# Diagonal of a 2-D prefix sum: rows kept in fp32, loaded uncast in 384-row strips, three rows per partition added before the matmul

## The chip, the cores and the metric

The kernel runs on one core of one Trainium2 chip. The metric is the device time in microseconds (us), lower is better; a time quoted for a kernel is the median of its runs.

The profiles show one execution each. Their span, from the first to the last instruction, is shorter than the time of the same run, and the profile before is of a run of 667.14 us, below the median; so spans are compared with spans and times with times.

## The reference

```python
def setup_inputs():
    B, H, W = 4, 4224, 4224
    return {"x": np.random.randn(B, H, W).astype(np.float32)}

def reference(x):
    ps = np.cumsum(np.cumsum(x, axis=1), axis=2)
    diag = np.diagonal(ps, axis1=1, axis2=2)
    return np.cumsum(diag, axis=1).astype(np.float32)
```

Element i of the diagonal is the sum of the square x[:i+1, :i+1], and the output is a running sum of that: 4 x 4224 numbers out of 285.5 MB. Every element of x has to be read once; the rest is adding. Rows left of the diagonal enter as row sums, columns above it as column sums, and the blocks on the diagonal are split by a triangular mask.

## The kernel before

Four matrices are read in strips of 768 rows (six rows per partition), cast from fp32 to bf16 by the DMA on GpSimd's queue, into three buffers. TensorE adds up columns: a one-hot selector `sel` puts the 128 partitions' sum into one row of a PSUM tile `d`, one matmul for each of the six rows and each 384 columns. VectorE masks the diagonal block and makes the row sums next to it; ScalarE makes the row sums further left (`act_sum`).

```python
    def load_rows(o, b, r0):
        f = o.shape[1]
        nc.gpsimd.dma_start(
            out=o, in_=x[b, r0 : r0 + f * P, :].rearrange("(p f) w -> p f w", f=f)
        )
    # ... (cut)
        def add_up(strip, f, r0, acc, um, wp=0, ws=None):
            # ... (cut)
            for j in range(g + nw, NG):
                for q in range(f):
                    columns(j, 0, GW, strip[:, q, j * GW : (j + 1) * GW])
            # ... (cut)
            block = strip[:, :, r0:hi]
            nc.vector.tensor_mul(out=mu, in0=block, in1=um)
            nc.vector.tensor_sub(out=block, in0=block, in1=mu)
            for q in range(f):
                for h in range(nw):
                    columns(g + h, 0, GW, mu[:, q, h * GW : (h + 1) * GW])
                if ws > wp:
                    act_sum(acc[:, q, 0:1], strip[:, q, wp:ws])
            row_sums(acc[:, :, 1], strip[:, :, ws:hi])
```

In the tail (the last 384 rows, in pieces) bf16 matmuls with an identity (`fold_in`) add up columns for VectorE, before the fp32 matmuls `fin_a`, `fin_b` and `fin_e` weigh the last sums together:

```python
        fold_in(fold_a, part_a, *acuts[1], 256)
        row_sums(asum[:, :, 3], fold_a)
        arows = last.tile([P, 2], FP32, name="arows")
        row_sums(arows, asum)
```

Of the kernel before, what the change touches and what calls it, by code (L numbers as in the profile page):

```python
# [8 lines left out]
FP32 = mybir.dt.float32  # L9
# [8 lines left out]
def kernel(  # L18
# [14 lines left out]

    nc = tc.nc
# [5 lines left out]
    F2 = 2 * F  # L40
# [7 lines left out]
    NS = NG // 2  # L48
# [17 lines left out]


    HC = GW
    NH = N - HC
    src = x[LB, T0:N, :].rearrange("(h p) w -> p h w", p=P)  # L70
    src_a = src[:, 0:2, :]
    head = last.tile([P, F, HC], FP32, name="head")
    nc.sync.dma_start(out=head, in_=src[:, :, NH:N])

    def strip_tile():
        return strips.tile([P, F2, N], BF16, name="strip")

    def load_rows(o, b, r0):
        f = o.shape[1]
        nc.gpsimd.dma_start(  # L80
            out=o, in_=x[b, r0 : r0 + f * P, :].rearrange("(p f) w -> p f w", f=f)
        )

    prefetched = []
    for i in range(NBUF):
        t = strip_tile()
        load_rows(t, 0, i * F2 * P)
        prefetched.append(t)


    sel = consts.tile([P, 2 * NW - 1], BF16, name="sel")
    nc.vector.memset(sel, 0.0)
    nc.vector.memset(sel[:, NW - 1 : NW], 1.0)

    um_all = consts.tile([P, (F2 * F2 + F * F + F) * P], BF16, name="um")
    nc.vector.memset(um_all, 1.0)  # L96

    def upper_mask(f, c0):

        um = um_all[:, c0 : c0 + f * f * P].rearrange("p (q c) -> p q c", q=f)  # L100
        nc.gpsimd.affine_select(  # L101
            out=um,
            in_=um,
            compare_op=ALU.is_gt,
            fill=0.0,
            base=0,
            pattern=[[-1, f], [1, f * P]],
            channel_multiplier=-f,
        )
        return um  # L110

    um6 = upper_mask(F2, 0)
    um3 = upper_mask(F, F2 * F2 * P)
    um1 = um_all[:, (F2 * F2 + F * F) * P :]
    nc.gpsimd.affine_select(
        out=um1,
        in_=um1,
        compare_op=ALU.is_gt,
        fill=0.0,
        base=0,  # L120
        pattern=[[1, GW]],
        channel_multiplier=-1,
    )

    ones_all = consts.tile([P, P + 1 + GW], FP32, name="ones_all")
    nc.vector.memset(ones_all, 1.0)
    ident = ones_all[:, :P]
    ones_col = ones_all[:, P : P + 1]
    ones_row = ones_all[:NW, P + 1 :]
# [9 lines left out]

    HP = P // 2  # L140
    halves = consts.tile([P, HP], FP32, name="halves")
    nc.gpsimd.tensor_add(out=halves, in0=ident[:, :HP], in1=ident[:, HP:])

# [78 lines left out]
    ident_h = consts.tile([P, P], BF16, name="ident_h")  # L222
    nc.vector.tensor_copy(out=ident_h, in_=ident)

# [5 lines left out]
    weights4_h = consts.tile([P, P], BF16, name="weights4_h")  # L230
    nc.vector.tensor_copy(out=weights4_h, in_=weights4)

    def fold_in(o, src, c0, c1, w, start=False):

        for c in range(c0, c1, w):
            matmul(o, ident_h, src[..., c : c + w], start=start and c == c0)

    def act_sum(acc, src):
        w = src.shape[-1]
        dump = dumpool.tile([P, 2176], BF16, name="dump")  # L240
# [7 lines left out]
    pairs = []  # L248

    def pair_sum(acc, src):  # L250

        w = src.shape[-1] // 2
        pair = last.tile([P, 288], FP32, name=f"pair{len(pairs)}")
        pairs.append(pair)
# [8 lines left out]
        )  # L263

# [11 lines left out]
    def scalar_cols(r0):  # L276

        return r0 * 9 // 16 // 32 * 32



    rows6, rows3 = [], []
    for i, n in enumerate((NW, NG)):
        rows6.append(consts.tile([P, n + 1, F2], FP32, name=f"rows6_{i}"))
        rows3.append(consts.tile([P, n, F], FP32, name=f"rows3_{i}"))
        nc.vector.memset(rows6[i], 0.0)
        nc.vector.memset(rows3[i], 0.0)


    asum = last.tile([P, 2, 4], FP32, name="asum")  # L290
# [262 lines left out]
```

## Time and profile before

| | before |
|---|---|
| time, median of the first 3 runs | 668.9 us (667.1 to 668.97) |
| span of the profile | 665.4 us |
| read from HBM | 285.47 MB |
| last full strip of 384 rows landed | 648.76 us |
| VectorE busy, instructions counted | 326.4 us, 136 |

The lines on which the prediction rests are in it, below. The order of reading is: which engine or queue is full, then the chain of waits for what releases what, then the tail.

### The profile page before, as it was taken

How to read it: one execution, taken by the hardware profiler on the slowest of the kernel's cores; microseconds unless marked ns; L12 is line 12 of the kernel's file. 1: busy time of each engine (PE TensorE's matmuls, PEld its weight loads, DVE VectorE, ACT ScalarE, POOL GpSimd, SP SyncE). 2: the span in 40 equal slices, each digit the busy share in tenths (PEclk: the TensorE clock that was granted, in tenths of full speed). 3: DMA queues.
4: the chain of work that ended last, by engine and by line, in shares of the span. 5: the costliest groups of instructions: out<-in, count | busy, mean ns of one | idle time of the engine just before them, and what ended most of it. 6: DMA issues, size and time to landing. Idle time of an engine off the chain costs nothing.

```text
span 665.4 us, 2461 instructions
## 1 busy us (share of the span) xinstructions
PE 201.7 (30%) x948; PEld 103.7 (16%) x948; DVE 326.4 (49%) x136; ACT 136.9 (21%) x222; POOL 31.8 (5%) x62
## 2 busy tenths in 40 slices
PE   0081423402007143140200623404032163250418
PEld 0040211201004021120100312202011031120103
DVE  3261625456906153454780524436388243352767
ACT  0001121406300103040630020304063002030434
POOL 6100000000000000000000000000000000001000
PEclk9995857656558585666755957666565586766758
DMA  9999999999999999999999999999999999999998
GB/s 206 219 219 219 219 219 215 212 210 218 219 218 219 219 220 218 218 213 212 216 218 218 217 219 219 218 219 211 215 216 219 219 214 220 216 219 216 214 208 162
DMA packets 7631, 143.25 MB, mean 215 GB/s; under 512 B 536, under 2 KB 1604, under 8 KB 2116
## 3 DMA queue, kind: packets, MB, share of 16 engines
q0 software_dynamic: 7152, 142.44, 99.9%
q1 hardware_dynamic: 468, 0.66, 0.3%
q8 instruction: 7, 0.11, 0.1%
q14 instruction: 4, 0.03, 0.0%
HBM read 285.47 MB, written 0.07 MB: 429 GB/s over the span
## 4 chain that ended last, share of the span: by engine, by line
another core or an unknown queue 44%; DVE 42%; DMA 11%; issue 1%; POOL 0%; PE 0%; DVEq 0%; POOLq 0%
DVE acc L246 27%; DMA strip<-in_x_dram 11%; DVE mu L333 7%; DVE strip L334 7%; DVE c L440 0%; POOL strip L411 0%; DVE rows L348 0%; PE d L226 0%; POOL strip L400 0%; DVE pu L246 0%; PE fin_e L226 0%; DVE c L266 0%; DVE pair L255 0%; PE carry_ps L226 0%
## 5 line engine op out<-in xcount | busy, mean ns | idle before, releaser
L226 PE MATMUL d<-strip,sel 128*33 128x384 bf16 (+1 forms) x603 | 140.7, 408 | 397.9 <-DMA strip<-in_x_dram 397.9
L241 ACT ACTIVATE dump<-strip 128x416 bf16<-128x416 bf16 (+6 forms) x110 | 125.1, 1138 | 520.5 <-DMA strip<-in_x_dram 517.8
L333 DVE TENSOR_TENSOR mu<-strip,um 128x4608 bf16<-128x4608 bf16 (+1 forms) x24 | 52.4, 2183 | 316.4 <-DMA strip<-in_x_dram 316.3
L246 DVE TENSOR_REDUCE acc<-strip 128x6 f32<-128x4608 bf16 (+6 forms) x23 | 196.0, 8523 | 0.8
L226 PEld LDWEIGHTS <-sel 128*33 128x33 bf16 (+1 forms) x849 | 94.9, 112 | 534.1 <-issue 495.9
L226 PE MATMUL d<-mu,sel 128*33 128x384 bf16 (+1 forms) x243 | 48.9, 353 | 45.4 <-DVE mu L333 45.4
L334 DVE TENSOR_TENSOR strip<-strip,mu 128x4608 bf16<-128x4608 bf16 (+1 forms) x24 | 52.4, 2183 | 1.0
L80 POOL DMA_DIRECT2D strip<-in_x_dram x24 | 16.5, 687 | 536.7 <-DVE acc L246 312.3
L241 ACT ACTIVATION_READ_ACCUMULATOR dump<-strip 128x1 f32 x110 | 20.5, 186 | 0.0
L226 PE MATMUL fold<-strip,ident_h 128*128 128x480 bf16 x8 | 3.4, 601 | 10.8 <-DMA strip<-in_x_dram 10.8
L96 DVE MEMSET um<- 128x6144 bf16 x1 | 5.2, 5178 | 1.2 <-issue 1.2
L216 DVE TENSOR_SCALAR steps<-steps 128x128 int32<-128x128 int32 x1 | 0.2, 227 | 11.0 <-POOL steps L215 11.0
L101 POOL TENSOR_SCALAR_AFFINE_SELECT um<-um 128x4608 bf16<-128x4608 bf16 (+1 forms) x2 | 5.2, 2614 | 4.0 <-DVE um L96 4.0
L226 PEld LDWEIGHTS <-ident_h 128*128 128x128 bf16 x21 | 2.2, 113 | 14.8 <-issue 13.8
L411 POOL DMA_DIRECT2D strip<-in_x_dram x5 | 2.7, 552 | 26.5 <-DMA strip<-in_x_dram 26.5
L226 PE MATMUL d<-ones_all,rows 128*33 128x128 f32 (+1 forms) x12 | 2.3, 347 | 5.4 <-DVE rows L348 5.4
L226 PE MATMUL fold_a<-strip,ident_h 128*128 128x512 bf16 x13 | 3.3, 380 | 0.3 <-DMA strip<-in_x_dram 0.3
L246 DVE TENSOR_REDUCE parts<-strip 128x3 f32<-128x3072 bf16 x1 | 3.4, 3352 | 0.0
L400 POOL DMA_DIRECT2D strip<-in_x_dram x2 | 1.4, 714 | 30.8 <-DVE acc L246 30.8
L226 PEld LDWEIGHTS d<-halves,rows 128*33 128x33 f32 (+1 forms) x24 | 2.5, 150 | 0.7 <-issue 0.5
L226 PE MATMUL d<-halves,rows 128*33 128x64 f32 (+1 forms) x24 | 2.6, 284 | 0.0
L348 DVE TENSOR_TENSOR rows<-acc 64x30 f32<-64x30 f32 (+2 forms) x12 | 2.1, 177 | 0.9
(80 smaller groups left out, 34.7 us busy)
## 6 DMA issues: line engine op xcount, KB each, us to landing
strip<-in_x_dram POOLq DMA_DIRECT2D x19, 6336.0 KB, 76.6
strip<-in_x_dram POOLq DMA_DIRECT2D x5, 3168.0 KB, 59.8
strip<-in_x_dram POOLq DMA_DIRECT2D x1, 1152.0 KB, 50.2
strip<-in_x_dram POOLq DMA_DIRECT2D x1, 768.0 KB, 53.3
strip<-in_x_dram POOLq DMA_DIRECT2D x3, 240.0 KB, 54.3
head<-in_x_dram SPq DMA_DIRECT2D x1, 576.0 KB, 4.0
strip<-in_x_dram POOLq DMA_DIRECT2D x1, 176.0 KB, 43.2
strip<-in_x_dram POOLq DMA_DIRECT2D x1, 64.0 KB, 28.6
```

What stands on the lines that cost most here:

```text
L80: nc.gpsimd.dma_start(out=o, in_=x[b, r0 : r0 + f * P, :].rearrange("(p f) w -> p f w", f=f))
L96: nc.vector.memset(um_all, 1.0)
L101: nc.gpsimd.affine_select(out=um, in_=um, compare_op=ALU.is_gt, fill=0.0, base=0, pattern=[[-1, f], [1, f * P]], channel_multiplier=-f,)
L216: nc.vector.tensor_single_scalar(out=steps, in_=steps, scalar=2, op=ALU.arith_shift_right)
L226: nc.tensor.matmul(o, lhsT=lhsT, rhs=rhs, start=start, stop=False, skip_group_check=True)
L241: nc.scalar.activation(out=dump[:, :w], in_=src, func=ACT.Copy, accum_out=acc)
L246: nc.vector.reduce_sum(out=acc, in_=src, axis=AX.X)
L333: nc.vector.tensor_mul(out=mu, in0=block, in1=um)
L334: nc.vector.tensor_sub(out=block, in0=block, in1=mu)
L348: nc.vector.tensor_add(out=o, in0=acc[..., 0], in1=acc[..., 1])
L400: nc.gpsimd.dma_start(out=part_a[:, :, c0:c1], in_=src_a[:, :, c0:c1])
L411: nc.gpsimd.dma_start(out=part_b[:, sb, c0:c1], in_=x[b, r0 : r0 + R, :NH].rearrange("r (k c) -> r k c", k=4)[:, :, c0:c1],)
```

## The change

The intent is to drop the cast and the software queue, and to keep full fp32 precision: SyncE loads strips of 384 rows (three rows per partition) as they are. An fp32 matmul takes more time for a column than a bf16 one (in the trace of before it is recorded twice, at 0.82 ns a column each, against 0.42 once), so VectorE adds the three rows first and TensorE then needs a third of the matmuls. The mask is made of -1 and 0, and a second selector, `minus_sel`, turns the sign.

```diff
     def load_rows(o, b, r0):
-        f = o.shape[1]
-        nc.gpsimd.dma_start(
-            out=o, in_=x[b, r0 : r0 + f * P, :].rearrange("(p f) w -> p f w", f=f)
+        nc.sync.dma_start(
+            out=o, in_=x[b, r0 : r0 + GW, :].rearrange("(p f) w -> p f w", f=F)
         )
 ... (cut)
-            for j in range(g + nw, NG):
-                for q in range(f):
-                    columns(j, 0, GW, strip[:, q, j * GW : (j + 1) * GW])
-            nc.vector.tensor_mul(out=mu, in0=block, in1=um)
-            nc.vector.tensor_sub(out=block, in0=block, in1=mu)
-            row_sums(acc[:, :, 1], strip[:, :, ws:hi])
 ... (cut)
+            for q in range(F):
+                act_sum(acc[:, k, q, 0:1], strip[:, q, :ws])
+            for q in range(F):
+                block = strip[:, q, g * GW : hi]
+                masked(mu[:, q, :], block, um3[:, q, :], acc[:, k, q, 2:3])
+            for q in range(1, F):
+                add_to(mu[:, 0, :], mu[:, q, :])
+            columns(g, mu[:, 0, :], minus_sel)
+            if hi < N:
+                for q in range(1, F):
+                    add_to(strip[:, 0, hi:], strip[:, q, hi:])
+                for j in range(g + 1, NG):
+                    columns(j, strip[:, 0, j * GW : (j + 1) * GW])
+            for q in range(F):
+                pair_sum(acc[:, k, q, 1:2], strip[:, q, ws:hi])
 ... (cut: in the tail)
-        fold_in(fold_a, part_a, *acuts[1], 256)
-        row_sums(asum[:, :, 3], fold_a)
+        sum_a(3, *acuts[1], acuts[1][0] + 768)
```

`sum_a` does with ScalarE and VectorE what the bf16 `fold_in` matmuls did.

More of the change, by code (lines that the diff above doesn't have):

```diff
@@ L39 @@
     F = 3
-    F2 = 2 * F
     GW = P * F
@@ L47 @@
     NBUF = 3
-    NS = NG // 2
     NW = NG * LB
@@ L64 @@
     ctx.enter_context(tc.manual_schedule())
-    HC = GW
-    NH = N - HC
-    src = x[LB, T0:N, :].rearrange("(h p) w -> p h w", p=P)
-    src_a = src[:, 0:2, :]
-    head = last.tile([P, F, HC], FP32, name="head")
-    nc.sync.dma_start(out=head, in_=src[:, :, NH:N])
     def strip_tile():
-        return strips.tile([P, F2, N], BF16, name="strip")
+        return strips.tile([P, F, N], FP32, name="strip")
     def load_rows(o, b, r0):
-        f = o.shape[1]
-        nc.gpsimd.dma_start(
-            out=o, in_=x[b, r0 : r0 + f * P, :].rearrange("(p f) w -> p f w", f=f)
+        nc.sync.dma_start(
+            out=o, in_=x[b, r0 : r0 + GW, :].rearrange("(p f) w -> p f w", f=F)
         )
@@ L86, with selector @@
         t = strip_tile()
-        load_rows(t, 0, i * F2 * P)
+        load_rows(t, 0, i * GW)
         prefetched.append(t)
-    sel = consts.tile([P, 2 * NW - 1], BF16, name="sel")
-    nc.vector.memset(sel, 0.0)
-    nc.vector.memset(sel[:, NW - 1 : NW], 1.0)
-    um_all = consts.tile([P, (F2 * F2 + F * F + F) * P], BF16, name="um")
-    nc.vector.memset(um_all, 1.0)
-    def upper_mask(f, c0):
-        um = um_all[:, c0 : c0 + f * f * P].rearrange("p (q c) -> p q c", q=f)
+    NH = N - GW
+    src = x[LB, T0:N, :].rearrange("(h p) w -> p h w", p=P)
+    src_a = src[:, 0:2, :]
+    head = last.tile([P, F, GW], FP32, name="head")
+    nc.sync.dma_start(out=head, in_=src[:, :, NH:N])
+    def selector(name, value):
+        t = consts.tile([P, 2 * NW - 1], FP32, name=name)
+        nc.vector.memset(t, 0.0)
+        nc.vector.memset(t[:, NW - 1 : NW], value)
+        return t
+    um3 = consts.tile([P, F, GW], BF16, name="um3")
+    um1 = consts.tile([P, GW], BF16, name="um1")
+    for um, pattern, cm in (
+        (um3, [[-1, F], [1, GW]], -F),
+        (um1, [[1, GW]], -1),
+    ):
+        nc.vector.memset(um, -1.0)
         nc.gpsimd.affine_select(
@@ L106, in upper_mask @@
             base=0,
-            pattern=[[-1, f], [1, f * P]],
-            channel_multiplier=-f,
-        )
-        return um
-    um6 = upper_mask(F2, 0)
-    um3 = upper_mask(F, F2 * F2 * P)
-    um1 = um_all[:, (F2 * F2 + F * F) * P :]
-    nc.gpsimd.affine_select(
-        out=um1,
-        in_=um1,
-        compare_op=ALU.is_gt,
-        fill=0.0,
-        base=0,
-        pattern=[[1, GW]],
-        channel_multiplier=-1,
-    )
-    ones_all = consts.tile([P, P + 1 + GW], FP32, name="ones_all")
+            pattern=pattern,
+            channel_multiplier=cm,
+        )
+    sel = selector("sel", 1.0)
+    minus_sel = selector("minus_sel", -1.0)
+    ones_all = consts.tile([P, P + GW], FP32, name="ones_all")
     nc.vector.memset(ones_all, 1.0)
     ident = ones_all[:, :P]
-    ones_col = ones_all[:, P : P + 1]
-    ones_row = ones_all[:NW, P + 1 :]
+    ones_row = ones_all[:NW, P:]
     nc.gpsimd.affine_select(
@@ L138 @@
     )
-    HP = P // 2
-    halves = consts.tile([P, HP], FP32, name="halves")
-    nc.gpsimd.tensor_add(out=halves, in0=ident[:, :HP], in1=ident[:, HP:])
     def counted(name, rows, width, pieces):
@@ L220 @@
     nc.vector.tensor_scalar_max(out=weights4, in0=steps, scalar1=0.0)
-    ident_h = consts.tile([P, P], BF16, name="ident_h")
-    nc.vector.tensor_copy(out=ident_h, in_=ident)
     def matmul(o, lhsT, rhs, start=False):
@@ L228, in matmul @@
         )
-    weights4_h = consts.tile([P, P], BF16, name="weights4_h")
-    nc.vector.tensor_copy(out=weights4_h, in_=weights4)
-    def fold_in(o, src, c0, c1, w, start=False):
-        for c in range(c0, c1, w):
-            matmul(o, ident_h, src[..., c : c + w], start=start and c == c0)
     def act_sum(acc, src):
         w = src.shape[-1]
-        dump = dumpool.tile([P, 2176], BF16, name="dump")
+        dump = dumpool.tile([P, 2688], BF16, name="dump")
         nc.scalar.activation(
@@ L246, in row_sums @@
         nc.vector.reduce_sum(out=acc, in_=src, axis=AX.X)
-    pairs = []
     def pair_sum(acc, src):
         w = src.shape[-1] // 2
-        pair = last.tile([P, 288], FP32, name=f"pair{len(pairs)}")
-        pairs.append(pair)
+        pair = dumpool.tile([P, 1024], BF16, name="pair")
         nc.vector.scalar_tensor_tensor(
@@ L263, in pair_sum, with add_to @@
         )
+    def add_to(o, i):
+        nc.vector.tensor_add(out=o, in0=o, in1=i)
     def masked(o, i, m, acc):
@@ L274, in masked @@
         )
-    def scalar_cols(r0):
-        return r0 * 9 // 16 // 32 * 32
-    rows6, rows3 = [], []
+    accs = []
     for i, n in enumerate((NW, NG)):
-        rows6.append(consts.tile([P, n + 1, F2], FP32, name=f"rows6_{i}"))
-        rows3.append(consts.tile([P, n, F], FP32, name=f"rows3_{i}"))
-        nc.vector.memset(rows6[i], 0.0)
-        nc.vector.memset(rows3[i], 0.0)
-    asum = last.tile([P, 2, 4], FP32, name="asum")
+        accs.append(consts.tile([P, n, F, 3], FP32, name=f"acc{i}"))
+        nc.gpsimd.memset(accs[i], 0.0)
+    asum = last.tile([P, 2, 5], FP32, name="asum")
     dtot = last.tile([P, F], FP32, name="dtot")
@@ L293, with do_head @@
     hu = last.tile([P, 3], FP32, name="hu")
-    hmu = last.tile([P, 3, GW], BF16, name="hmu")
-    row_sums(hs, head)
-    for h in range(F):
-        w = GW - h * P
-        masked(hmu[:, h, :w], head[:, h, HC - w :], um1[:, :w], hu[:, h : h + 1])
-    nc.vector.tensor_sub(out=dtot, in0=hs, in1=hu)
-    nc.gpsimd.tensor_copy(out=asum[:, :, 0], in_=dtot[:, 0:2])
+    hmu = last.tile([P, F, GW], FP32, name="hmu")
+    def do_head():
+        row_sums(hs, head)
+        for h in range(F):
+            w = GW - h * P
+            masked(
+                hmu[:, h, GW - w :], head[:, h, GW - w :], um1[:, :w], hu[:, h : h + 1]
+            )
+        for h in range(1, F):
+            add_to(hmu[:, 0, h * P :], hmu[:, h, h * P :])
+        nc.vector.tensor_add(out=dtot, in0=hs, in1=hu)
+        nc.vector.tensor_copy(out=asum[:, :, 0], in_=dtot[:, 0:2])
     for b in range(B):
         whole = b < LB
-        r6, r3 = rows6[b // LB], rows3[b // LB]
+        acc = accs[b // LB]
         if b in (0, LB):
@@ L311, in row_of, with columns @@
             return b * NG + j if whole else (j + 1) % NG
-        def columns(j, lo, hi, rhs):
+        def columns(j, rhs, s=sel):
             k = row_of(j)
-            lhsT = sel[:, NW - 1 - k : NW - 1 - k + rows]
-            matmul(d[:, lo:hi], lhsT, rhs, start=first[0])
+            matmul(d, s[:, NW - 1 - k : NW - 1 - k + rows], rhs, start=first[0])
             first[0] = False
-        def add_up(strip, f, r0, acc, um, wp=0, ws=None):
-            nw = f * P // GW
-            g = r0 // GW
-            hi = r0 + f * P
-            for j in range(g + nw, NG):
-                for q in range(f):
-                    columns(j, 0, GW, strip[:, q, j * GW : (j + 1) * GW])
-            if ws is None:
-                ws = scalar_cols(r0)
-            mu = mup.tile([P, f, f * P], BF16, name=f"mu{f}")
-            block = strip[:, :, r0:hi]
-            nc.vector.tensor_mul(out=mu, in0=block, in1=um)
-            nc.vector.tensor_sub(out=block, in0=block, in1=mu)
-            for q in range(f):
-                for h in range(nw):
-                    columns(g + h, 0, GW, mu[:, q, h * GW : (h + 1) * GW])
-                if ws > wp:
-                    act_sum(acc[:, q, 0:1], strip[:, q, wp:ws])
-            row_sums(acc[:, :, 1], strip[:, :, ws:hi])
@@ L342, with add_up @@
-        acc6 = smalls.tile([P, NS, F2, 2], FP32, name="acc6")
-        acc3 = smalls.tile([P, 2, F, 2], FP32, name="acc3")
-        nc.vector.memset(acc6[:, 0, :, 0], 0.0)
-        def sum_up(o, acc):
-            nc.vector.tensor_add(out=o, in0=acc[..., 0], in1=acc[..., 1])
-        ns = NS if whole else NS - 1
-        for s in range(ns):
+        def add_up(strip, g, ws):
+            k = row_of(g)
+            hi = (g + 1) * GW
+            mu = mup.tile([P, F, GW], FP32, name="mu")
+            for q in range(F):
[13 more added lines that the diff above has]
+                pair_sum(acc[:, k, q, 1:2], strip[:, q, ws:hi])
@@ L352 @@
+        for g in range(NG if whole else LG):
             strip = prefetched.pop(0) if prefetched else None
@@ L354 @@
                 strip = strip_tile()
-                load_rows(strip, b, s * F2 * P)
-            add_up(strip, F2, s * F2 * P, acc6[:, s], um6)
-            if not whole and s == 1:
-                for h in range(F):
-                    columns(LG, h * P, GW, hmu[:, h, : GW - h * P])
-        a6 = acc6[:, :ns]
-        for h in range(2):
-            ps = slice(h * HP, (h + 1) * HP)
-            k = row_of(h)
-            sum_up(r6[ps, k : k + 2 * ns : 2, :], a6[ps])
-        strip = strip_tile()
-        if whole:
-            load_rows(strip[:, :F], b, T0)
-            add_up(strip[:, :F], F, T0, acc3[:, 0], um3)
-            sum_up(r3[:, row_of(LG), :], acc3[:, 0])
-        else:
-            for h in range(2):
-                load_rows(strip[:, h * F : h * F + F], b, T0 - (2 - h) * GW)
-            add_up(strip[:, :F], F, T0 - 2 * GW, acc3[:, 0], um3)
-            sum_up(r3[:, row_of(LG - 2), :], acc3[:, 0])
-            fold_g = psum_s.tile([P, F, 160], FP32, name="fold")
-            wp, ws = 1280, 1280 + 1536
-            fold_in(fold_g, strip[:, F:], 0, wp, 160, start=True)
-            parts = last.tile([P, F, 3], FP32, name="parts")
-            add_up(strip[:, F:], F, T0 - GW, parts, um3, wp, ws)
-            row_sums(parts[:, :, 2], fold_g)
-            row_sums(r3[:, row_of(LG - 1), :], parts)
+                load_rows(strip, b, g * GW)
+            hi = (g + 1) * GW
+            add_up(strip, g, hi * 5 // 8 // 32 * 32)
+            if b == 0 and g == NBUF - 1:
+                do_head()
+            if not whole and g == 1:
+                columns(LG, hmu[:, 0, :], minus_sel)
         if b < LB - 1:
             continue
-        for q in range(F2):
-            matmul(d[:, q : GW : F2], r6[:, :rows, q], halves)
+        r3 = last.tile([P, rows, F], FP32, name=f"r3_{rows}")
+        row_sums(r3, acc)
         for q in range(F):
@@ L399 @@
             for c0, c1 in acuts:
-                nc.gpsimd.dma_start(out=part_a[:, :, c0:c1], in_=src_a[:, :, c0:c1])
+                nc.sync.dma_start(out=part_a[:, :, c0:c1], in_=src_a[:, :, c0:c1])
             CB = NH // 4
@@ L410 @@
                 r0 = TB + sb * R
-                nc.gpsimd.dma_start(
+                nc.sync.dma_start(
                     out=part_b[:, sb, c0:c1],
@@ L416, with sum_a @@
                 )
-            fold_a = psum_s.tile([P, 2, 256], FP32, name="fold_a")
-            c0, c1 = acuts[0]
-            cp, ca = c0 + 1792, c0 + 1792 + 256
-            fold_in(fold_a, part_a, c0, c0 + 1280, 256, start=True)
-            for h in range(2):
-                act_sum(asum[:, h, 1:2], part_a[:, h, cp:ca])
-            row_sums(asum[:, :, 2], part_a[:, :, ca:c1])
+            def sum_a(k, c0, c1, ca):
+                for h in range(2):
+                    act_sum(asum[:, h, k : k + 1], part_a[:, h, c0:ca])
+                for h in range(2):
+                    pair_sum(asum[:, h, k + 1 : k + 2], part_a[:, h, ca:c1])
+            sum_a(1, *acuts[0], acuts[0][0] + 1536)
         pu = last.tile([rows, 2], FP32, name=f"pu{rows}")
@@ L434 @@
         matmul(carry_ps[:, 1:2], apart, pu[:, 0:1])
-        if not whole:
-            fold_in(fold_a, part_a, c0 + 1280, cp, 256)
         carry = last.tile([rows, 2], FP32, name=f"carry{rows}")
@@ L448 @@
         if whole:
-            to = out[0:LB, :].rearrange("b (g i) -> (b g) i", i=GW)
-            nc.sync.dma_start(out=to, in_=c12[:, 1, :])
+            c12_w = c12
             continue
+        to = out[0:LB, :].rearrange("b (g i) -> (b g) i", i=GW)
+        nc.sync.dma_start(out=to, in_=c12_w[:, 1, :])
         nc.sync.dma_start(
@@ L482, in finish @@
             )
-        by_ps = psum_s.tile([P, P], FP32, name="fold")
-        for c in range(0, CB, P):
-            w = min(P, CB - c)
-            matmul(by_ps[:w], part_b[:, 0, c : c + w], weights4_h, start=c == 0)
-        by = last.tile([P, P], FP32, name="by")
-        nc.scalar.copy(out=by, in_=by_ps)
         weigh_b(dtot[:, 2:3], weights, M0, start=True)
@@ L494 @@
             weigh_a(arows[:, h : h + 1], h * P, start=h == 0)
-        weigh_b(ones_col, by, M0)
         for h in range(2):
             weigh_b(arows[:, h : h + 1], weights, h * P)
-        bsum = last.tile([P, 2, 2], FP32, name="bsum")
-        for k, ca in ((0, 480), (1, 416)):
-            act_sum(bsum[:, k, 0:1], part_b[:, k + 1, :ca])
-            pair_sum(bsum[:, k, 1:2], part_b[:, k + 1, ca:])
-        finish(fin_a, 0, M0)
-        for k in range(2):
+        bsum = last.tile([P, 3, 2], FP32, name="bsum")
+        for k, ca in ((0, 480), (1, 480), (2, 416)):
+            act_sum(bsum[:, k, 0:1], part_b[:, k, :ca])
+            pair_sum(bsum[:, k, 1:2], part_b[:, k, ca:])
+            if k == 1:
+                finish(fin_a, 0, M0)
+        for k in range(3):
             for i in (1, 0):
-                weigh_b(bsum[:, k, i : i + 1], weights4, M0 + (k + 1) * R)
+                weigh_b(bsum[:, k, i : i + 1], weights4, M0 + k * R)
         esum = last.tile([P, 3], FP32, name="esum")
```

## The prediction

> **What bounds the kernel now.** I read the summary of the span first, then the slices and the DMA queues, then the chain of waits in order of time, then the groups kept apart by shape, and last the timeline of the final 20 us.
>
> ```profile
> PE 201.7 (30%) x948; PEld 103.7 (16%) x948; DVE 326.4 (49%) x136; ACT 136.9 (21%) x222; POOL 31.8 (5%) x62
> ...
> DMA  9999999999999999999999999999999999999998
> ...
> q0 software_dynamic: 7152, 142.44, 99.9%
> q1 hardware_dynamic: 468, 0.66, 0.3%
> ...
> HBM read 285.47 MB, written 0.07 MB: 429 GB/s over the span
> ```
>
> No engine is busy for more than half of the span, while the 16 DMA engines are full in every slice. 142.44 MB were written (bf16) but 285.47 MB read (fp32), so the cast halves only the side that lands in SBUF. The chain of waits gives the rate:
>
> ```profile
> 1.33 33.28 DMA strip<-in_x_dram
> 34.64 2.57 DVE mu L333
> 37.23 2.57 DVE strip L334
> 39.83 4.95 DVE acc L246
> 44.78 19.74 another core or an unknown queue
> 64.62 2.57 DVE mu L333
> ...
> 364.70 2.57 DVE mu L333
> ...
> 529.11 2.57 DVE mu L333
> ```
>
> VectorE starts on a strip of 768 rows, works for 10 us, then waits 20 us until the next has landed; the wait that the chain calls an unknown queue is the one that the table of waits calls DVE mu waiting for DMA strip (316.3 us in 20 waits). From 364.70 to 529.11 one whole matrix goes by: 4224 x 4224 x 4 bytes = 71.37 MB in 164.41 us, which is 434.1 GB/s read. The half strips of 384 rows are no slower: one and a half strips take 44.87 us (155.25 to 200.12), one 29.9. So the end of the kernel is: first landing at 34.6, a stream at 434 GB/s, and what follows the last landing:
>
> ```profile
> 648.76 0.76 DVE L333 TENSOR_TENSOR mu<-strip,um 128x1152 bf16<-128x1152 bf16 x1 [5.42 <-DMA strip<-in_x_dram]
> ...
> 655.65 0.55 DVE L246 TENSOR_REDUCE pu<-d 11x1 f32<-11x384 f32 x1 [0.53 <-PE d L226]
> ...
> 662.33 0.38 DVE L255 SCALAR_TENSOR_TENSOR pair<-strip 128x208 f32<-128x208 bf16 x1
> ```
>
> The last strip lands at 648.7, the tail pieces behind it (13.6 us of stream) keep VectorE waiting for data until 662.3, and the span ends at 665.4: only 3 us lie after the last byte, 16.7 us after the last strip.
>
> **What the Trainium skill says.** "DMA: Bandwidth & Descriptors", section "Where 436 GB/s comes from", puts the ceiling of the 16 engines' ports at 435.2 GB/s. The trace agrees: 434.1 on the read side, so there is nothing left to gain in the stream. The trace does not show a long stream that also writes at that rate, since the cast writes half. The same page, section "iDMA fabric", has a load stream from the SyncE queue, alone, at 408.7 GB/s, with 1 MiB per DMA and rows of 4 KiB. Here one 6.5 MB DMA has 50,688 contiguous bytes per partition; if the missing 6% is a cost per row or per DMA, it shrinks to well under 1%; if it is the price of writing what is read, it stays. "VectorE: DVE Perf Modes", section "The perf-mode tier table", gives an fp32 tensor_tensor one element per cycle, against two in bf16; the second is in the trace (1152 bf16 in 758 ns, 4608 in 2558: 0.52 ns each and 158 ns fixed). "Vector Engine (DVE) Microarchitecture Reference", section "Points that are easy to get wrong", says that the scalar-tensor-tensor form with two SBUF sources that are not bf16 runs at half rate; no such instruction is in the trace (the mask is bf16, pairs are bf16), so this is open.
>
> **The change part by part.** The bytes read stay the same. Loads go from 24 strip DMAs on the GpSimd queue to 43 on the SyncE queue, 6.49 MB each, 6.49/434 = 14.95 us each. Three buffers of 50,688 bytes per partition hold three such strips, as before in bytes, so the stream runs 30 us ahead of the strip at work instead of 60. What a strip g (0 to 10) now costs must fit in 14.95 us per engine, and its buffer must be free 29.9 us after it landed.
>
> ```profile
> L226 PE MATMUL d<-strip,sel 128*33 128x384 bf16 x450 | 104.7, 407 | 320.0 <-DMA strip<-in_x_dram 320.0
> ...
> L246 DVE TENSOR_REDUCE acc<-strip 128x6 f32<-128x10752 bf16 x4 | 45.4, 11353 | 0.1
> ...
> L241 ACT ACTIVATE dump<-strip 128x2144 bf16<-128x2144 bf16 x9 | 17.9, 1990 | 13.4 <-DMA strip<-in_x_dram 13.2
> ...
> L266 DVE SCALAR_TENSOR_TENSOR hmu<-head,um 128x384 bf16<-128x384 f32 x1 | 0.5, 547 | 0.0
> ...
> L226 PE MATMUL fin_a<-weights,arows 128*1 128x256 f32 x2 | 0.6, 377 | 0.2 <-DVE arows L246 0.2
> ...
> L226 PE MATMUL fin_a<-weights,arows 128*1 128x128 f32 x2 | 0.4, 272 | 0.0
> ```
>
> VectorE loses the reductions (196 us) and the bf16 mask multiply and subtract (105 us). One element costs 1.042 ns (the reductions of 4608 and 10752 differ by 6400 ns) and an instruction about 157 ns. Per strip it gains: three masked products, 3 x (0.547 + 0.08 accumulator read) = 1.9; two adds of 384, 2 x 0.557 = 1.1; two adds of 3840-384g, for g=0 2 x 4.157 = 8.3; three pair sums of 80 to 800, 0.24 x 3 = 0.7 at g=0 plus 0.24 for reads, 3.2 at g=10. Sum 12.3 us at g=0, 9.4 at g=5, 6.2 at g=10; at half rate of the pair sums 12.5, 10.8, 8.7. All under 14.95. Over the kernel: 81 + 48 + 189 + 88 and 15 of small work, about 420 us, or 478 at half rate.
>
> ScalarE: a sum over ws costs 0.833 ws + 0.39 us with its read; three of 2624 make 7.7 us, the kernel some 205 us.
>
> TensorE: fp32 matmuls appear twice each in the trace, at 0.82 ns per column (377-272 over 128), twice the 0.42 of bf16, so four bf16 passes. In the first strip 66 bf16 matmuls took 13.6 us at a granted clock of 0.75, 0.155/clock each; fp32 then is 0.62/clock, 0.94 us at the mean clock 0.66 and 1.24 at 0.5. But VectorE first adds three rows, so their number falls from 846 to 264, at most 11 per strip: 10.3 to 13.6 us. PE busy would be 200 to 270 us. The buffer of strip 0 is free at 3 + 8.3 + 10 x 0.94 = 21 us after landing, 24 at the low clock, so the next load is queued 6 to 9 us before the queue runs dry. Nothing here enters the path.
>
> GpSimd loses 20 us of issuing, off the path. At the start SyncE issues at 0.8 instead of 1.3; the head load (issued 0.8, landed 4.0 us later, of which 1.4 is bytes) shows some 2.2 us of latency, so strip 0 lands near 18.0. The rest of the stream, 279.0 MB, ends at 660.8 at 434 GB/s (before: 662.3).
>
> The tail is where work reaches the path. After the last strip lands at T, VectorE now does in order: that strip (g=9: 1.9+1.1+1.1+3.0 = 7.1), the sum of parts and matmuls (1.4), pair sums of the tail (1.3), pu and mask (1.2), carry (0.6), two scans (2.05), pair sums (1.5), three short pairs and an add (2.0), two pairs (0.8), the last matmuls, add and store (1.2). It ends near T+18.2; the tail pieces land by T+14.5. So VectorE, not the last byte, ends it: 1.5 us later than the 16.7 of before, 5 at half rate. T is 660.8-13.6 = 647.2, the span 665.4 or 669. Times are 3.5 us above the span (668.9 against 665.4; the profiled run itself 1.7). That makes 669 to 672 at an unchanged rate; at 430 GB/s, 6 more.
>
> **Rivals.** (1) The stream loses where it also writes 434 GB/s. At 425: 285.5/0.425 is 14 us more, so about 684; at 408.7 it is 41 us more, 711. For it: no margin at the port ceiling, and the skill's figure. Against it: its rows are a twelfth of these, and the head load, also fp32 and uncast in 1,536-byte rows, took 40.4% of 5 us x 16 engines for 0.59 MB, 292 GB/s, above the 217 that the cast stream writes, so writing is not bounded there. (2) VectorE or the four-pass matmuls become the bound on early strips, or hold buffers longer than 29.9 us. At 12.5 against 14.95 it would take 20% more than reckoned; then only strips 0 and 1 of each matrix would exceed it, some 1 to 3 us each, up to 10 us in all. (3) The cast or the software queue costs something now and its loss speeds the stream up. Against it: 434.1 of 435.2 leaves 0.3%, 2 us. (4) All is hidden and the time is unchanged to 0.5%, the case reckoned above.
>
> **Range and chances.** Most weight is on 668 to 676; a moderate loss of rate (425 to 430) puts 676 to 684; a fifth I give to a loss that exceeds 2% (above 682.3). I put 673, and 664 to 694 to hold it 8 times in 10. Faster by over 2% would need 655.5, less than the read side allows: 0.02. Within 2%: 0.77. Slower: 0.21.
>
> **What would show each step.** DMA again 9 in all slices, and starts of successive strips 14.95 us apart: rate kept; 15.3 or more with DMA still full: rival 1. DVE at 63% (or 72%: half rate, seen in pair sums of 720 at 1.66 us rather than 0.91). PE under 45%, and waits of SyncE's loads for PE or DVE that end before the queue is empty; DMA slices under 9 would mean rival 2. Strip 0 landing at 18. Some 18 to 22 us from the last strip's landing to the end, with VectorE busy throughout. The prediction fails if long fp32 rows stream below 425 GB/s or a strip needs over 14.95 us on one engine.

## More of the kernel before

On the page of before, the columns are packets, MB and the share of 16 engines' time:

```profile
q8 instruction: 7, 0.11, 0.1%
q14 instruction: 4, 0.03, 0.0%
```

They bring the engines' own instructions, in pieces of 16,384 bytes (q8) and 8,192 bytes (q14).

## The result, and the profile after

The changed kernel took 677.26 us (676.84 to 677.95, 4 runs) against 668.05 for the kernel before in the same rounds. A ratio is the mean time of one kernel's fast runs over that of the other's fast runs of the same rounds, so it isn't quite the ratio of these medians: 1.0139, with a 95% interval of 1.0118 to 1.016. That is within 2%, but it is a real loss of 9 us.

The page of the kernel after:

```profile
span 675.7 us, 2520 instructions
...
PE 281.8 (42%) x576; PEld 70.3 (10%) x576; DVE 387.9 (57%) x738; ACT 198.0 (29%) x275; POOL 7.1 (1%) x30
...
DMA  9999999999999999999999999999999999999993
...
q1 hardware_dynamic: 7924, 285.55, 98.2%
...
q14 instruction: 10, 0.08, 0.0%
HBM read 285.47 MB, written 0.07 MB: 423 GB/s over the span
```

The DMA engines are still full up to the last slice, which reads 3 where before it read 8; and VectorE is over half busy at most. So the stream still bounds the kernel, but it moves fewer bytes per us over the span (423 against 429 GB/s), and the end is longer. To see where, one follows the landings. ScalarE waits for each strip in this kernel, so its starts are the landings. The timeline of ScalarE, after (start, duration, what; in brackets the idle time before and what ended it):

```profile
276.89 1.59 ACT L214 ACTIVATE dump<-strip 128x1664 bf16<-128x1664 f32 x1 [10.45 <-DMA strip<-in_x_dram]
...
292.86 1.80 ACT L214 ACTIVATE dump<-strip 128x1920 bf16<-128x1920 f32 x1 [10.86 <-DMA strip<-in_x_dram]
...
307.85 1.99 ACT L214 ACTIVATE dump<-strip 128x2144 bf16<-128x2144 f32 x1 [9.24 <-DMA strip<-in_x_dram]
...
655.68 2.20 ACT L214 ACTIVATE dump<-strip 128x2400 bf16<-128x2400 f32 x1 [8.75 <-DMA strip<-in_x_dram]
```

From 292.86 to 307.85 is 14.99 us, and nearly all strips are that far apart: 6.49 MB in 14.99 us, 433 GB/s. But from 276.89 to 292.86 is 15.97 us. Six of the 42 intervals are such long ones, ending near 66, 172, 293, 414, 520 and 626 us (the first also holds the head load). The last strip lands at 655.68 instead of 648.76, 6.9 us later.

What happened in the long intervals is in the trace's single DMA packets. They don't name their engine, so I chained them: a packet that starts within 20 ns of another's end is taken to be on the same engine, which gives 16 chains. One of these chains around 282 us, from my own listing of the records:

```
start us   took      bytes   queue
280.088   1875 ns   50688   q1
281.959    325 ns    8192   q14   (instructions)
282.272   2534 ns   50688   q1
284.803   1874 ns   50688   q1
```

An instruction piece takes 0.33 us of that engine, and the data packet behind it takes 0.66 us longer than its neighbours: 0.98 us lost on one of 16 engines, which is the excess of the interval. Pieces at 55.1, 161.0, 282.0, 402.9, 508.8 and 614.7 us lie on the same chain, each with a packet of 2534 or 2535 ns behind it. A strip is there only when all 16 engines have brought their share, so this engine's delays add up: at the end its last packet of the last strip ends at 655.06 us, those of the other 15 chains between 648.6 and 650.5. Pieces of the other engines fall on other chains, one or two each, and stay inside that lag. (In the kernel before, the pieces are spread over different chains, as far as the chaining there can be trusted.)

The Trainium skill, "Runtime: NRT & Kernel Launch", section "Instruction fetch mechanics", says that each engine's instruction memory is a queue which is refilled in blocks by a DMA queue of the sequencer, and takes the cost as mostly hidden from the engine. The trace agrees on the engine: no wait of VectorE is put down to it. What it shows in addition is that the stream of data pays. The spacing fits VectorE: the trace has 795 instructions on it with those for semaphores, and 795 / 128 is 6.2 pieces (8,192 bytes for 128 instructions is the skill's proportion, 16 KiB for 256).

After the last strip, the chain of waits of the kernel after (start, duration, the engine and tile that the end waited for):

```profile
655.68 2.31 ACT dump L214 x2
...
662.66 0.26 DVE r L219
...
668.73 0.17 DVE arows L219
...
668.94 1.44 PE fin_a L207 x4
670.38 2.79 PE fin_b L207 x16
...
673.58 0.18 DVE ye L449
```

and its counterpart in the chain of the kernel before:

```profile
663.29 0.18 DVE ye L521
```

The end comes 2.1 us after `ye` in both (the store). In the kernel after, the three sums of ScalarE hold the first 7.0 us, VectorE the next 6.1, then TensorE 4.6 until `ye`. The windows of both kernels tell why TensorE is slow there. The columns are us, then busy time and count of PE, PEld, DVE, ACT and POOL, then PE's granted clock, the DMA share and GB/s. After, then before:

```profile
666.00:669.00 3.00, 0.06 (x1) 0.06 (x2) 2.83 (x8) 2.91 (x7) 0.00 (x0) 0.50 0.09 32
669.00:672.00 3.00, 3.00 (x13) 1.53 (x14) 2.08 (x11) 1.41 (x6) 0.00 (x0) 0.50 0.01 4
```

```profile
658.00:661.00 3.00, 2.79 (x19) 1.33 (x19) 2.45 (x6) 0.96 (x3) 0.00 (x0) 1.00 1.13 204
```

TensorE did next to nothing from 666 to 668.94 and then ran at clock 0.50; before, it was busy with the bf16 folds and ran at 1.00. Also, the DMA share is 0.09 and 0.01 here: the data had ended but for the engine that lagged.

The difference of the spans, 675.7 - 665.4 = 10.3 us, as I add it up (the parts make 10.5):

| part | us | how |
|---|---|---|
| start | 0.85 | two strips were in at 34.13 and the head's bytes took 1.36 more; before, the same bytes were in at 34.64 |
| rate | 1.9 | 42 strips x (14.99 - 14.945) |
| instruction pieces | 4.4 | 636.55 - 42 x 14.99 - 1.36 = 5.6 in the stretch from strip 0 to the last, against 1.2 of irregular intervals before |
| tail | 3.4 | 20.0 us from the last strip's landing to the end, against 16.6 |

### The profile page after: what moved, and what is told of

Read it like the earlier page. It is cut to its first block, busy times and chain, and to the rows that moved or that the text cites. A ratio compares the mean times of both kernels' runs of the same rounds, so it can differ in the third digit from the quotient of the medians.

```text
span 675.7 us, 2520 instructions
## 1 busy us (share of the span) xinstructions
PE 281.8 (42%) x576; PEld 70.3 (10%) x576; DVE 387.9 (57%) x738; ACT 198.0 (29%) x275; POOL 7.1 (1%) x30
## 4 chain that ended last, share of the span: by engine, by line
DMA 72%; DVE 13%; PE 11%; ACT 2%; issue 1%; SPq 0%; DVEq 0%; ACTq 0%
DMA strip<-in_x_dram 72%; PE d L207 10%; DVE strip L236 8%; DVE mu L239 2%; ACT dump L214 2%; DVE mu L236 2%; PE fin_b L207 0%; DVE pair L225 0%; DVE c L377 0%; PE fin_a L207 0%; SPq L69 0%; DVE c L239 0%; DVE pu L219 0%; DVE yl L416 0%; DVE r L219 0%
## 5 line engine op out<-in xcount | busy, mean ns | idle before, releaser
L214 ACT ACTIVATE dump<-strip 128x224 bf16<-128x224 f32 (+13 forms) x137 | 184.0, 1343 | 453.4 <-DMA strip<-in_x_dram 450.4
L207 PE MATMUL d<-strip,sel 128*33 128x384 f32 (+1 forms) x440 | 223.3, 677 | 130.6 <-DVE strip L236 130.6
L239 DVE SCALAR_TENSOR_TENSOR mu<-strip,um 128x384 f32<-128x384 f32 x129 | 65.2, 555 | 265.0 <-DMA strip<-in_x_dram 265.0
L236 DVE TENSOR_TENSOR strip<-strip 128x3840 f32<-128x3840 f32 (+9 forms) x80 | 188.4, 2355 | 1.4
L207 PE MATMUL d<-mu,minus_sel 128*33 128x384 f32 (+1 forms) x86 | 51.9, 698 | 249.6 <-DVE mu L236 249.6
L207 PEld LDWEIGHTS d<-strip,sel 128*33 128x33 f32 (+1 forms) x440 | 58.2, 140 | 301.6 <-DVE strip L236 170.5
L225 DVE SCALAR_TENSOR_TENSOR pair<-strip 128x80 bf16<-128x80 f32 (+12 forms) x138 | 81.7, 592 | 3.2
L236 DVE TENSOR_TENSOR mu<-mu 128x384 f32<-128x384 f32 x86 | 47.8, 556 | 1.5
L225 DVE DVE_READ_ACCUMULATOR pair<-strip 128x1 f32 x138 | 11.3, 82 | 0.0
L239 DVE DVE_READ_ACCUMULATOR mu<-strip,um 128x1 f32 x129 | 10.7, 83 | 0.0
```

The source lines that it names most:

```text
L207: nc.tensor.matmul(o, lhsT=lhsT, rhs=rhs, start=start, stop=False, skip_group_check=True)
L214: nc.scalar.activation(out=dump[:, :w], in_=src, func=ACT.Copy, accum_out=acc)
L225: nc.vector.scalar_tensor_tensor(out=pair[:, :w], in0=src[:, :w], scalar=1.0, in1=src[:, w:], op0=ALU.mult, op1=ALU.add, accum_out=acc,)
L236: nc.vector.tensor_add(out=o, in0=o, in1=i)
L239: nc.vector.scalar_tensor_tensor(out=o, in0=i, scalar=1.0, in1=m, op0=ALU.mult, op1=ALU.mult, accum_out=acc,)
```

## The experiments

The theory is that VectorE's instructions, fetched through an engine that carries data, delay the stream, and that TensorE's clock lengthens the tail. The rivals: the price of writing every byte that is read (the prediction's own), the SyncE queue, and VectorE's busy time itself. All nine kernels gave right results. Each ratio is to the kernel before in the same call: 667.52 us for e1, e2, e3 and e5, 667.33 for e4, e6 and e7, 667.27 for e8 and e9.

### e1_many: 18 tiny VectorE instructions more on each strip

```diff
             for q in range(F):
                 pair_sum(acc[:, k, q, 1:2], strip[:, q, ws:hi])
+            if not (b == LB and g == LG - 1):
+                for i in range(18):
+                    nc.vector.memset(idle[:, i : i + 1], 0.0)
```

> The changed kernel with 18 tiny VectorE memsets (one column each) more per strip, 756 in all, some 1.1 us of VectorE time per strip. Theory 1 (VectorE's own instructions are fetched in pieces of 8 KB, some 128 instructions, always through the same DMA engine, and each piece holds up that engine's data by 0.98 us): about 6 more such pieces, the strip intervals of 16 us come about every fourth strip instead of every seventh or eighth, the last strip lands near 661.5 instead of 655.7, time 683 (ratio to the changed kernel about 1.009, to the kernel before about 1.022). Theory 2 (the uncast stream of the SyncE queue itself loses rate, by byte or by DMA): landings as before, time 677. Theory 3 (VectorE's work slows the loads by its time or traffic): later too, and the next run as well.

It took 683.42 us, ratio 1.023 (1.0212 to 1.0248). ScalarE's timeline and the DMA view:

```profile
248.75 1.19 ACT L214 ACTIVATE dump<-strip 128x1184 bf16<-128x1184 f32 x1 [11.64 <-DMA strip<-in_x_dram]
...
264.70 1.40 ACT L214 ACTIVATE dump<-strip 128x1440 bf16<-128x1440 f32 x1 [12.04 <-DMA strip<-in_x_dram]
...
661.22 2.21 ACT L214 ACTIVATE dump<-strip 128x2400 bf16<-128x2400 f32 x1 [9.71 <-DMA strip<-in_x_dram]
```

```profile
q14 instruction: 16, 0.13, 0.0%
```

Intervals of 15.95 us now come at about every fourth strip. (795 + 756) / 128 makes 12 pieces, and 12 are found with a stretched packet behind; they go on one chain, though two chains that end within a few ns of each other can be mixed up there. The last strip lands at 661.22, 5.5 us later than in the kernel after, for six more pieces: 0.92 us each.

### e2_one: the same VectorE time in one instruction

```diff
+            if not (b == LB and g == LG - 1):
+                nc.vector.memset(idle, 0.0)      # [128, 1056] bf16
```

> Control of the run before: one VectorE memset of about the same time (1056 columns, some 1.1 us) per strip instead of 18 tiny ones. Theory 1: no further instruction pieces worth speaking of (42 instructions, a third of one), last strip at 655.7 to 656.7, time 677 to 678. Theory 2: 677. Theory 3: as late as the run with 18 tiny ones, 683.

It took 677.63 us, ratio 1.0147 (1.013 to 1.0164), as the kernel after does. ScalarE's timeline:

```profile
655.67 2.20 ACT L214 ACTIVATE dump<-strip 128x2400 bf16<-128x2400 f32 x1 [8.74 <-DMA strip<-in_x_dram]
```

The last strip landed at 655.67 (655.68 in the kernel after), with six pieces on the chain. So e1's loss comes from the number of instructions and not from VectorE's time.

### e3_lean: fewer VectorE instructions for the same result

```diff
-            for q in range(F):
-                masked(mu[:, q, :], block, um3[:, q, :], acc[:, k, q, 2:3])
-            for q in range(1, F):
-                add_to(mu[:, 0, :], mu[:, q, :])
-            columns(g, mu[:, 0, :], minus_sel)
+            nc.vector.tensor_mul(out=mu, in0=strip[:, :, g * GW : hi], in1=um3)
+            row_sums(acc[:, k, :, 2], mu)
+            for q in range(F):
+                columns(g, mu[:, q, :], minus_sel)
 ... (cut)
-            for q in range(F):
-                pair_sum(acc[:, k, q, 1:2], strip[:, q, ws:hi])
+            row_sums(acc[:, k, :, 1], strip[:, :, ws:hi])
```

The very last strip keeps the old form, so that the tail is the same.

> The changed kernel with the same sums in fewer VectorE instructions: one multiply and one reduction for the masked block instead of three products with accumulators, no adding of the three masked rows (TensorE takes them as three matmuls), one reduction for the pair sums; the last strip of all keeps the products and pair sums. About 5 instructions and 2 waits per strip instead of 17 or 18. Theory 1: 2 or 3 pieces of VectorE's instructions instead of 6, so the last strip lands 3 to 4 us earlier, at 652 to 653, time 673.5 to 674.5. Theory 2: last strip at 655.7, time 677. Theory 3: VectorE's time per strip is nearly the same, so 677.

It took 673.63 us, ratio 1.0084 (1.0064 to 1.0103). VectorE has 274 counted instructions instead of 738, but is busy for longer: 434.1 us against 387.9. The timeline and the DMA view:

```profile
652.23 2.21 ACT L214 ACTIVATE dump<-strip 128x2400 bf16<-128x2400 f32 x1 [8.70 <-DMA strip<-in_x_dram]
```

```profile
q14 instruction: 7, 0.06, 0.0%
```

The last strip lands 3.45 us earlier; two pieces with a 2534-ns packet behind are left on data (115.2 and 446.0 us). Four pieces fewer at 0.98 would be 3.9; a little is given back. Here TensorE's pieces come into the path too: besides the interval with the head load, only those that end at 96.5, 456.9 and 562.3 us are long (15.57, 15.55 and 15.42), and the first and the last of them follow q8 pieces at 86.9 and 552.7. More busy time and less total time: the rival "VectorE's busy time" is out.

### e5_gpsimd: the uncast loads on GpSimd's queue

```diff
-        nc.sync.dma_start(
+        nc.gpsimd.dma_start(        # load_rows, part_a and part_b
```

> The changed kernel, fp32 and uncast as it is, but with the loads issued by GpSimd's queue as in the kernel before. Theory 1: VectorE still fetches 6 pieces; if what a piece costs does not depend on the queue of the data, the last strip lands at 655 and the time stays at 676 to 678. Theory 2 in the form that the SyncE queue loses rate: strip intervals back to 14.95 and no intervals of 16, time about 670. Theory 2 in the form that writing as much as is read loses rate: 677 with intervals of 14.99.

It took 677.06 us, ratio 1.0137 (1.0119 to 1.0154). The timeline of ScalarE:

```profile
655.38 2.20 ACT L214 ACTIVATE dump<-strip 128x2400 bf16<-128x2400 f32 x1 [8.72 <-DMA strip<-in_x_dram]
```

The same six pieces have the same packets of 2534 ns behind them, and the regular interval is 14.99 to 15.00 us here too. So neither the long intervals nor the 0.3% of rate belong to the queue. With the queue ruled out, the 14.99 against 14.945 us goes with the uncast form (twice the bytes written); no run separates the cast from the size of the packets (50,688 bytes written against 25,344).

### e4_before_many: many VectorE instructions in the kernel before

```diff
             row_sums(acc[:, :, 1], strip[:, :, ws:hi])
+            if ws is not None and r0 < T0 - 2 * GW:
+                for i in range(48):
+                    nc.vector.memset(idle[:, i : i + 1], 0.0)
```

Edited from the kernel before. Does the cast stream suffer in the same way? 768 instructions were added here.

> The kernel before with 48 tiny VectorE memsets after each of 16 full strips, 768 in all (as many as the run with 18 per strip added to the changed kernel), 2.9 us per strip inside VectorE's idle 15 to 20 us. Theory 1 (a piece of VectorE's instructions holds up one DMA engine): 6 more pieces. If a piece costs there the 0.98 us of the uncast stream, the last strip lands some 4 to 6 us later and the time is 672 to 674. If the data packet behind a piece is not stretched in the cast stream (the trace of the kernel before shows no stretched packet behind its 8 KB pieces, which take 0.32 us), 1 to 2 us: 668.5 to 670. If the instructions cost nothing in a stream that a queue two strips deep keeps fed: 667.5.

It took 669.65 us, ratio 1.0039 (1.0024 to 1.0054), 2.3 us more. VectorE's timeline and the DMA view:

```profile
651.25 0.76 DVE L334 TENSOR_TENSOR mu<-strip,um 128x1152 bf16<-128x1152 bf16 x1 [4.84 <-DMA strip<-in_x_dram]
```

```profile
q14 instruction: 10, 0.08, 0.0%
```

The last strip lands 2.5 us later. Here a piece takes 0.32 us and the 25,344-byte packet behind it 2098 ns instead of 1886: 0.53 us a piece, about half of the uncast price. Seven pieces on one chain make 3.7 us, and 1.2 of that the kernel before already pays elsewhere (estimates from these packets; 2.5 is left, and 2.5 was measured). So the mechanism isn't tied to fp32, to SyncE's queue or to the new kernel; uncast data pays about double.

### e6_warm: idle matmuls to keep TensorE's clock up in the tail

```diff
+    def warm(n):
+        for i in range(n):
+            matmul(warm_ps, warm_in[:, :P], warm_in[:, P:], start=True)
 ... (cut: for the last matrix only)
+            warm(10)     # before the sum of r3
+            warm(10)     # before pu
+            warm(24)     # behind the carry matmuls
```

The matmuls multiply bf16 zeros into a PSUM tile that nobody reads.

> The changed kernel with 44 idle bf16 matmuls into an unused PSUM tile in the last 15 us (10 ahead of the parts' matmuls, 10 after them, 24 after the carry), so that TensorE's clock does not fall to a half there. If the tail is set by TensorE at half clock after the sums of the rows (4.5 us from 668.94 to 673.47, records of 0.2 us instead of 0.1): 1.5 to 2 us shorter, time 675.3 to 675.8. If VectorE's and ScalarE's work or the last landing sets it: 677 to 677.5. The landing of the last strip stays at 655.7 in both.

It took 677.23 us, ratio 1.0146 (1.0131 to 1.0161): no gain, a miss. The chain of waits says why:

```profile
664.77 1.73 PE warm_ps L207 x10
...
666.67 4.01 PE warm_ps L207 x24
```

The idle matmuls themselves are now on the path: 1.73 us ahead of the carry, 4.01 us ahead of the last matmuls, which start at 670.7 instead of 668.9. The clock was up (1.00), and from the last sums to the end it took 5.6 us instead of 7.0, which the later start used up. The run speaks for the clock's part in the tail, but shows no gain from it; a smaller dose had to be tried.

### e7_lean_warm: e3 and e6 together

The edit is e3's and e6's.

> The version with few VectorE instructions, with the idle matmuls in the tail too. If the two losses add up: 673.6 - 1.5 to 2 = 671.6 to 672.1, still 0.6% above the kernel before, since the uncast stream needs 14.99 us per strip against 14.95 and the tail after the last strip stays some 18 us against 16.7. If the tail is set by something else: 673.6.

It took 672.83 us, ratio 1.008 (1.0063 to 1.0097). Against e3's 673.63, in another call, 0.8 us is gained, or 0.0004 of the ratios, which the intervals don't separate: unclear.

### e8_warm2: fewer idle matmuls

```diff
-            warm(10)     # before the sum of r3
-            warm(10)     # before pu
-            warm(24)     # behind the carry matmuls
+            warm(6)      # before the sum of r3
+            warm(18)     # behind the carry matmuls
```

Against e6.

> The changed kernel with idle bf16 matmuls in the tail again, but placed so that none delays a needed one: 6 while ScalarE finishes the last strip, none between the parts' matmuls and the carry (there 10 of them pushed the carry back by 1.1 us in the run before), 18 after the carry. If half clock in the last sums costs the time: from the sums of the rows to the end 5.6 us instead of 7.0, nothing given back, time 1.2 to 1.5 us below the changed kernel, 675.8 to 676.1. If it is given back again: 677.

It took 675.39 us (675.28 to 676.03), ratio 1.0122 (1.0107 to 1.0137): all four runs are below the fastest of the kernel after, by 1.9 us in the medians. These come from two calls, though; by the ratios to the kernel before it is 0.0017, or 1.1 us, and their intervals overlap. The chain of waits:

```profile
669.33 0.82 PE fin_a L207 x4
...
672.01 0.18 DVE ye L461
```

From `fin_a` to `ye` is 2.7 us, against 4.6 in the kernel after (the profile is of the slowest of the four runs, 676.03); the granted clock in these windows is 1.00 instead of 0.50. So some 1 to 2 us of the tail's excess of 3.4 us was TensorE's clock.

### e9_lean_warm2: e3 and e8 together

The edit is e3's and e8's.

> The version with few VectorE instructions, with the idle matmuls placed in the same way: the two gains add, 673.6 - 1.2 to 1.5 = 672.1 to 672.4, against 672.8 with the first placing. Still above the kernel before (667 to 669): the uncast stream at 14.99 us per strip and two remaining instruction pieces put the last strip at 652.2 against 648.8, and the work behind it takes 1.5 to 2 us longer.

It took 671.54 us, ratio 1.0062 (1.0045 to 1.0079). That is 5.7 us better than the kernel after by the medians (5.1 by the ratios) and the best fp32 version tried, still 4.3 us behind the kernel before. Against e3 the same idle matmuls gain 2.1 us by the medians, 1.5 by the ratios. Its profiled execution was also its slowest run (673.18), in which `fin_a` waited for the idle matmuls, so the dose isn't robust. No version tried beat the kernel before.

## Why the prediction was right and wrong

The time, 677.3 us, lies in the range of 664 to 694 and within 2% of before, as given most weight; the estimate of 673.0 was 4.3 too low. The span reckoned at an unchanged rate was 665.4; it was 675.7. That the range held is partly luck: the working itself gave 669 to 672, and the room above it was meant for a loss of rate (425 to 430 GB/s) that didn't come; instruction pieces and the tail, which were not in it, filled that room. Some of the 669 to 672 was luck too: the step from span to time, 3.5 us, set the profile of a run of 667.14 against a median of 668.9, where the same run differs by 1.7. By its own steps:

- **The rate holds at 14.95 us per strip: nearly.** It was 14.99 wherever nothing disturbed. Rival 1, the price of writing what is read, is there, if that is what e5's rate shows, but at 0.3% or 1.9 us, not at 425 or 408.7 GB/s. The prediction's test for it misleads if it is read by the mean: that was 15.15 with DMA full, over halfway from 14.95 to the 15.3 that was to mean rival 1, and the cause was another. The single intervals show it.
- **The step that failed** is "the stream at 434 GB/s ends at 660.8", hence the last strip at 647.2. It landed at 655.68, 8.5 us later: 1.1 from the start, 1.9 from the rate, 5.6 from instruction pieces (rounded parts). The last term was missing in the sum altogether: GpSimd's saved issuing was counted, and VectorE's 600 additional instructions were priced in VectorE's time alone. Runs e1, e2 and e3 show that their number moves the landing: 2 pieces 652.23 (with TensorE's pieces in the path too), 6 pieces 655.68 (and 655.67), 12 pieces 661.22.
- **The tail of 18.2 us: mis-sized, within the 18 to 22 given.** It was 20.0. The prediction's own terms add up to 19.15, not 18.2, and up to `arows`, the second of the pair sums, to T+15.15; `arows` came at T+13.05. What follows it was reckoned at 4.0 us and took 7.0: the store's 2.1 us were put into a term of 1.2, and TensorE's last matmuls took 4.6 us at half clock. "VectorE busy throughout" was wrong: ScalarE held the first 7 us, TensorE the last 4.6. Run e8 brings some 1 to 2 us of this back by the clock.
- **Pair sums at half rate: no.** The group kept apart by shape:

```profile
L225 DVE SCALAR_TENSOR_TENSOR pair<-strip 128x720 bf16<-128x720 f32 x12 | 10.9, 906 | 0.3
```

The mean of one is 906 ns; at the 1.042 ns an element and 157 ns an instruction that the prediction read from the trace it would be 907, as its full-rate branch had it (0.91 us).
- **VectorE at 63%, TensorE under 45%: right side.** They were 57% and 42% (281.8 us, just over the 200 to 270 given). The queue never ran dry: loads were issued 32 us ahead of their landing by the median, so rival 2 is out.
- **Strip 0 at 18.0:** 19.13. The prediction's own 4.0 less 1.4 is a latency of 2.6 us, not 2.2, so 18.4; and the first packets of the engines took 2.2 to 3.5 us instead of 1.87.
- **Rival 3,** a gain from the lost cast or software queue, is out: uncast strips are 14.99 us apart and not under 14.945, and with GpSimd's queue (e5) the time is 677.06.

What stays open: why the packet behind a piece is stretched by 0.66 us, and why VectorE's pieces fall on one DMA engine each time. The assignment to engines is inferred from start and end times, not recorded; e1 and e3 support what follows from it, not the assignment itself. Of the tail's 3.4 us, 1 to 2 are shown to be the clock; the rest, ScalarE's and VectorE's sums in place of the folds, is argued from the chain.

## What to carry to other kernels

When a kernel is bounded by a DMA stream that fills all its engines, count VectorE's instructions as a cost to the stream and not only to that engine: here 128 of them cost 0.98 us, 0.53 beside the cast stream, and merging three small ones into one large one paid even where the engine then was busy for longer. TensorE's pieces also have stretched packets behind them (2340 to 2421 ns), but no run varied their number alone. A change that takes work from TensorE can cost it its clock for the few matmuls that end the kernel, here 0.50 instead of 1.00. If a stream fills all 16 DMA engines from start to end, as here, a change beside it can hardly gain, and its small costs at start, in stream and at the end are what to add up.

## What the Trainium skill lacked or had wrong

- "Runtime: NRT & Kernel Launch", section "Instruction fetch mechanics": it gives blocks of 16 KiB for each engine. Here VectorE's pieces are of 8,192 bytes (six for 795 instructions, twelve for 1,551), while q8, whose number follows TensorE's work (4 pieces in the kernel after and 7 in the kernel before, which have 1,152 and 1,896 matmuls and weight loads, or 4.5 and 7.4 times 256), has pieces of 16,384. The pieces don't name their engine; they are assigned by these counts.
- No page gives the cost of these fetches to a full data stream: 0.98 us a piece on one DMA engine for uncast data (0.33 for the piece, 0.66 for the packet behind), 0.53 for the cast stream, and VectorE's pieces in the changed kernel all on one engine, so that they add up (the engine inferred by chaining): 2, 6 and 12 pieces put the last landing at 652.2, 655.7 and 661.2 us.
- "Vector Engine (DVE) Microarchitecture Reference", section "Points that are easy to get wrong": half rate for the scalar-tensor-tensor form with two SBUF sources that aren't bf16 was not seen; 128x720 fp32 with an accumulated sum took 906 ns.
- "DMA: Bandwidth & Descriptors", section "iDMA fabric": its 408.7 GB/s for a SyncE load stream is for rows of 4 KiB. With 50,688 contiguous bytes per partition the stream ran at 433 GB/s, from SyncE's queue and from GpSimd's alike.
